# The first mLSTM head's q, k and v projections moved in front of the convolution tiles of a hybrid decoder step

## The chip, the cores and the metric

One core of a Trainium2 chip runs the whole step in one launch. The metric is the device time of a launch in microseconds (us), as the median of several runs; lower is better. The core has five engines that run at once, each with its own in-order instruction queue: TensorE (PE in the profile; PEld is its weight load), VectorE (DVE), ScalarE (ACT), GpSimd (POOL) and SyncE (SP, which here only issues DMAs).

## What is computed

One layer of a decoder for 512 prompt tokens and 8 x 8 sample tokens, so 576 columns of width 1024. Three groups of heads read the same normalised, modulated input; one output projection joins them, and an MLP follows. Cut to what matters:

```python
hn = (rmsnorm(x, norm1_w) * (1.0 + sc1) + sh1)           # sc, sh, g from adaLN of c
u = hn @ w_in
z, xbc, dt_raw, q, k, v, o, ig, fg, xr, gr = split(u)
xbc = silu(causal_conv(xbc, sconv0, w, b))               # 12 tiles of 128 channels
y_ssd = rmsnorm((ssd_chunked(xbc, softplus(dt_raw)) + xs * d) * silu(z))
hm = mlstm_chunked(q, k * 128 ** -0.5, v, ig, log_sigmoid(fg))   # 4 heads of 128
y_ml = rmsnorm(hm) * sigmoid(o)
y_lru = lru_scan(causal_conv(xr)) * gelu(gr)
x = x + g1 * (concat(y_ssd, y_ml, y_lru) @ w_out)
hn = rmsnorm(x, norm2_w) * (1.0 + sc2) + sh2
x = x + g2 * (square(relu(hn @ mlp_up)) @ mlp_down)
y = rmsnorm(x, final_norm_w)
```

All recurrent states are outputs too.

## The kernel before

Activations lie with channels on the 128 partitions and the 576 tokens along the free axis, in tiles from a pool of 54 places (`T`). A weight matrix is cut into 124 blocks of 1024 x 128; the host packs them in the order in which the kernel uses them, which it reads from the constant `ORDER`. For precision each block is split into two parts, `wh` (a copy on ScalarE, L150) and `wl` (the rest, L152, on POOL for blocks 7 to 32 and on VectorE for the others); each product is three matmuls (`mm_k`, L164), for two halves of 288 columns: 48 matmuls for a block of 8 k-steps. Raw blocks come by DMA on SP's queue (`w_load`, L128) into three buffers.

`unit` does one block: it loads and splits ahead, issues the matmuls into a pair of PSUM banks (`PG`, two pairs), calls `slot` after four k-steps, then the block's evacuation `evac`, then `slot` again. `slot` takes one step of each generator in `self.active`; the generators hold the work beside the projections: `gate_rows` (the gates' cumulative sums and maxima over tokens, mostly VectorE, up to a set of transposes at L596), `ssd(g)` (eight heads of the state space part, a chunk of 128 tokens in two steps), `mlstm(h, q, k, v)` (one mLSTM head), `ada_gen` (the later adaLN products) and others.

Evacuations differ. `ev_conv` (tiles of x, B and C, called "c") copies PSUM with three ScalarE operations (L611, L613, L614) into one of four row buffers `r`, scales on ScalarE into a second one (L620), adds three shifted products on VectorE (L626), a tanh on ScalarE (L649), and two VectorE operations give the result (L651, L653). `ev_copy` (q, k, v) is one ScalarE copy into a tile (L902). `ev_gates` starts `gate_rows` before the first of these blocks.

`start` does blocks 1 to 3 (tiles c8, c10, c0). `run` then does c1, c2, c3 (blocks 4 to 6), starts `ssd(0)`, and goes through `ORDER`: there "c" is a convolution tile, "m" the three blocks of an mLSTM head, "z", "x", "g" and "o" gate and recurrent-unit blocks. The first entries are c9 c11 c4 c5 c6 m0 c7 m1. An "m" appends the head's generator when its three blocks are done; when the last convolution is done `ssd(1)` is appended; `ada_gen` is appended at entry number `ADA_AT`. `ssd(0)` begins its chunks when `gate_rows` and its six convolution tiles are done. The head's first work is a broadcast load of `scr_nm` (L909, on SP's queue), then products of q and k.

The code only gives the order in which instructions are emitted. The final order in each engine's queue is drawn at build time by a scheduler that keeps dependences and buffers and models the instructions' times.

Of the kernel before, what the change touches and what calls it, by code (L numbers as in the profile page):

```python
# [67 lines left out]
class Kernel:  # L68
# [1200 lines left out]
    def run(self):  # L1269
# [11 lines left out]
        def inp(evac):  # L1281
            nonlocal blk
            self.unit([(blk, k, self.hn[k]) for k in range(KT)], evac)
            blk += 1
# [5 lines left out]
        convs = {9, 11, 4, 5, 6, 7}  # L1290
        for n, (kind, i) in enumerate(ORDER):
            if n == ADA_AT:
                self.active.append(self.ada_gen())
            if kind == "c":
                inp(lambda pg: self.ev_conv(pg, i))
                convs.remove(i)
                if not convs:
                    self.active.append(self.ssd(1))
            elif kind == "m":
                t = {}  # L1300
                inp(lambda pg: t.__setitem__("q", self.ev_copy(pg, "q")))
                inp(lambda pg: t.__setitem__("k", self.ev_copy(pg, "k", sc)))
                inp(lambda pg: t.__setitem__("v", self.ev_copy(pg, "v")))
                self.active.append(self.mlstm(i, t["q"], t["k"], t["v"]))
            elif kind == "x":
                if i == 0:
                    self.active.append(self.lru_setup())
                inp(lambda pg: self.ev_xr(pg, i))
                if i == 3:
                    self.active.append(self.lru())  # L1310
            elif kind == "g":
                inp(lambda pg: self.ev_gr(pg, i))
            elif kind == "z":
                if i == 0:
                    self.active.append(self.ssd_norm())
                inp(lambda pg: self.ev_z(pg, i))
            else:
                inp(lambda pg: self.ev_o(pg, i))
# [154 lines left out]
TODO = {0: [(0, 0)], 1: [(0, 1), (1, 0), (1, 1)], 2: [(0, 2), (1, 2)], 3: [(0, 3), (1, 3)], 4: [(0, 4), (1, 4), (2, 0), (2, 1)], 5: [(0, 5), (1, 5), (2, 2), (2, 3)], 6: [(0, 6), (1, 6), (2, 4), (2, 5)], 7: [(0, 7), (1, 7), (2, 6), (2, 7)]}  # L1473
GATES_FIRST = False
LOOKAHEAD = 4
ORDER = [(t[0], int(t[1:])) for t in "c9 c11 c4 c5 c6 m0 c7 m1 m2 z0 z1 x0 x1 x2 z3 z2 x3 g0 g1 z6 g2 g3 m3 z7 z5 z4 o0 o1 o2 o3".split()]
ADA_AT = 1
ON_ACT = ('mc_s', 'ssm_p', 'ssm_s')
PREP = 2
W_BUFS = 3  # L1480
# [23 lines left out]
def _layout(a):  # L1504
# [21 lines left out]
    blocks = [xt[8], xt[10], xt[0], xt[1], xt[2], xt[3]]  # L1526
    for kind, i in ORDER:
        blocks += [qt[i], kt[i], vt[i]] if kind == "m" else [{"c": xt, "x": rt, "g": gt, "z": zt, "o": ot}[kind][i]]
# [110 lines left out]
```

## Time and profile before

| | |
|---|---|
| three runs | 993.74, 996.15, 996.48 us (median 996.15) |
| the profiled execution | 995.4 us, of which its span, first to last instruction, 993.6 |
| granted TensorE clock, mean over the span | 0.987 |
| matmuls of line L164 in the chain that ended last | 66% of the span |
| HBM traffic | 119 GB/s over the span |

The profile is of one execution. "Busy" is the time in which an engine had an instruction in work; matmuls are pipelined, so a busy TensorE is not one at its peak. An idle time is put down to what ended it. A row of a timeline has the start, the length, the engine, the line, the operation, output and inputs and a count; in brackets, the idle time before it and what it waited for. In the page's rows of digits each digit is the busy share, in tenths, of one of 40 equal slices of 24.8 us.

### The profile page before, as it was taken

How to read it: one execution, taken by the hardware profiler on the slowest of the kernel's cores; microseconds unless marked ns; L12 is line 12 of the kernel's file. 1: busy time of each engine (PE TensorE's matmuls, PEld its weight loads, DVE VectorE, ACT ScalarE, POOL GpSimd, SP SyncE). 2: the span in 40 equal slices, each digit the busy share in tenths (PEclk: the TensorE clock that was granted, in tenths of full speed). 3: DMA queues.
4: the chain of work that ended last, by engine and by line, in shares of the span. 5: the costliest groups of instructions: out<-in, count | busy, mean ns of one | idle time of the engine just before them, and what ended most of it. 6: DMA issues, size and time to landing. Idle time of an engine off the chain costs nothing.

```text
span 993.6 us, 18146 instructions
## 1 busy us (share of the span) xinstructions
PE 959.5 (97%) x7369; PEld 904.1 (91%) x7370; DVE 590.2 (59%) x1180; ACT 399.8 (40%) x741; POOL 203.8 (21%) x220
## 2 busy tenths in 40 slices
PE   8999789889999999999999999999999999999996
PEld 5889778777788899999999999999999999999996
DVE  4669897887788377468444455533553355335544
ACT  3454744453646674345222234312441144114320
POOL 2836454532355532020000000000000000000032
PEclk8999999998999999999999999999999999999998
DMA  9721254654464333444222322222222222222202
GB/s 343 294 86 64 81 186 133 246 173 137 131 223 153 105 137 129 140 131 162 91 98 105 110 86 84 74 79 84 85 86 85 86 85 76 76 83 85 85 23 96
DMA packets 51220, 119.62 MB, mean 120 GB/s; under 512 B 6956, under 2 KB 17468, under 8 KB 51136
## 3 DMA queue, kind: packets, MB, share of 16 engines
q1 hardware_dynamic: 47024, 111.06, 32.7%
q10 hardware_dynamic: 3744, 6.85, 1.8%
q8 instruction: 58, 0.95, 0.4%
q0 software_dynamic: 368, 0.55, 0.2%
q14 instruction: 26, 0.21, 0.1%
HBM read 108.68 MB, written 9.76 MB: 119 GB/s over the span
## 4 chain that ended last, share of the span: by engine, by line
PE 76%; DVE 10%; ACT 4%; issue 3%; DMA 1%; POOL 0%; POOLq 0%; DVEq 0%; ACTq 0%
PE g L164 66%; DVE r L626 3%; PE adap L218 1%; PE g L1363 1%; DMA nmb<-scr_nm 1%; PE py L729 1%; PE lg L1129 1%; DVE att L707 1%; PE ps L734 1%; PE py L732 1%; DVE nmb L924 1%; DVE xbc L651 0%; DVE sp_e L494 0%; PE adas L228 0%; ACT r L620 0%
## 5 line engine op out<-in xcount | busy, mean ns | idle before, releaser
L150 ACT ACTIVATE wh<-raw 128x1024 fp32r<-128x1024 f32 x123 | 130.1, 1058 | 333.9 <-PE g L164 309.4
L164 PE MATMUL g<-hnh,wh 128*128 128x288 f32 x688 | 153.1, 302 | 10.1 <-ACT r L614 8.0
L164 PE MATMUL g<-hnh,wl 128*128 128x288 f32 x688 | 152.1, 299 | 0.6 <-DVE wl L152 0.6
L164 PE MATMUL g<-hnl,wh 128*128 128x288 f32 x688 | 151.8, 299 | 0.0
L152 DVE TENSOR_TENSOR wl<-raw,wh 128x1024 fp32r<-128x1024 f32 x97 | 118.7, 1225 | 29.5 <-ACT wh L150 29.4
L164 PEld LDWEIGHTS g<-hnh,wh 128*128 128x128 f32 x688 | 110.4, 189 | 19.3 <-ACT r L614 9.2
L164 PEld LDWEIGHTS g<-hnh,wl 128*128 128x128 f32 x688 | 111.6, 189 | 2.7 <-issue 1.2
L164 PEld LDWEIGHTS g<-hnl,wh 128*128 128x128 f32 x688 | 111.7, 189 | 0.8 <-issue 0.4
L164 PE MATMUL g<-h2h,wh 128*128 128x288 f32 (+1 forms) x512 | 110.9, 297 | 0.0
L164 PE MATMUL g<-h2l,wh 128*128 128x288 f32 (+1 forms) x512 | 110.9, 298 | 0.0
L164 PE MATMUL g<-h2h,wl 128*128 128x288 f32 (+1 forms) x512 | 110.0, 296 | 0.0
L307 DVE SCALAR_TENSOR_TENSOR xr<-g,modt,xr 128x288 f32<-128x288 f32 x38 | 19.7, 518 | 141.2 <-PE g L164 141.2
L164 PE MATMUL g<-hh,wl 128*128 128x288 f32 x480 | 102.9, 295 | 0.0
L164 PE MATMUL g<-hh,wh 128*128 128x288 f32 x480 | 102.5, 295 | 0.0
L164 PE MATMUL g<-hl,wh 128*128 128x288 f32 x480 | 102.4, 295 | 0.0
L1405 POOL TENSOR_SCALAR xr<-xr,vec 128x576 f32<-128x576 f32 (+2 forms) x8 | 15.2, 1900 | 383.8 <-ACT sqa L1237 363.4
L152 POOL TENSOR_TENSOR wl<-raw,wh 128x1024 fp32r<-128x1024 f32 x26 | 69.0, 2653 | 80.3 <-ACT wh L150 61.4
L164 PEld LDWEIGHTS g<-h2h,wl 128*128 128x128 f32 x512 | 83.4, 188 | 0.0
L164 PEld LDWEIGHTS g<-h2h,wh 128*128 128x128 f32 x512 | 83.1, 189 | 0.1
L164 PEld LDWEIGHTS g<-h2l,wh 128*128 128x128 f32 x512 | 83.0, 188 | 0.0
L164 PEld LDWEIGHTS g<-hh,wh 128*128 128x128 f32 x480 | 77.0, 188 | 0.0
L164 PEld LDWEIGHTS g<-hh,wl 128*128 128x128 f32 x480 | 77.0, 188 | 0.0
(399 smaller groups left out, 1652.7 us busy)
## 6 DMA issues: line engine op xcount, KB each, us to landing
raw<-w SPq DMA_DIRECT2D x124, 512.0 KB, 3.5
ada<-ada SPq DMA_DIRECT2D x32, 512.0 KB, 5.6
ada<-ada SPq DMA_DIRECT2D x32, 256.0 KB, 5.9
cumb<-scr_cum SPq DMA_DIRECT2D x16, 256.0 KB, 5.6
s<-s SPq DMA_DIRECT2D x16, 256.0 KB, 4.7
ssm_s<-s ACTq DMA_DIRECT2D x16, 256.0 KB, 2.9
x<-x SPq DMA_DIRECT2D x8, 288.0 KB, 4.7
xr<-x SPq DMA_DIRECT2D x8, 288.0 KB, 3.9
```

Of the source, the lines that this page charges most:

```text
L150: nc.scalar.activation(hi, raw, AF.Copy)
L152: eng.tensor_tensor(lo, raw, hi.bitcast(FT), op=OP.subtract)
L164: self.nc.tensor.matmul(pg.h[h][:m, :e], w(k), xx[:, h * HALF:h * HALF + e], start=start and n == 0, stop=stop and n == 2)
L218: nc.tensor.matmul(ps[32 * j:32 * j + 32, :256], self.cs[:, k, :], ks(k), start=k < 4, stop=k >= 4)
L307: self.nc.vector.scalar_tensor_tensor(dst[:, :HALF], pg.h[0][:, :HALF], gate[:, 0:1], x[:, :HALF], op0=OP.mult, op1=OP.add)
L626: nc.vector.scalar_tensor_tensor(a[:, :n], r[:, j:j + n], wcols[:, j:j + 1], a[:, :n], op0=OP.mult, op1=OP.add)
L707: self.eng("att").tensor_scalar(E[:, h * 128:(h + 1) * 128], cums[h2][:, h * 128:(h + 1) * 128], self.col1[:, c, hd:hd + 1], 0.0, op0=OP.a ...
L729: nc.tensor.matmul(o, xdt[:, h * 64:(h + 1) * 64], att[h // 4][:, hs], start=True, stop=not c)
L732: nc.tensor.matmul(o, S[:, h * 64:(h + 1) * 64], ce[h // 4][:, hs], start=False, stop=True)
L734: nc.tensor.matmul(pst, cb[:, 128:256], xend[:, :512], start=True, stop=True)
L924: self.eng("nmb").tensor_scalar(E[:, tk(c)], nmb[:, tk(c)], ecol(c), 0.0, op0=OP.add, op1=OP.min)
L1405: self.eng("fin").tensor_scalar(x, x, self.v("fnw")[:, o:o + 1], None, op0=OP.mult)
```

## The change

The head's three blocks become the first entry of `ORDER`, the head's generator is not started when they are done but after c6 (the entry after which it started before), and `ada_gen` is appended before the first entry, not before the second.

```diff
             if kind == "c":
                 inp(lambda pg: self.ev_conv(pg, i))
                 convs.remove(i)
+                if i == M0_AFTER:
+                    self.active.append(self.mlstm(*first))
                 if not convs:
                     self.active.append(self.ssd(1))
             elif kind == "m":
...
                 inp(lambda pg: t.__setitem__("v", self.ev_copy(pg, "v")))
-                self.active.append(self.mlstm(i, t["q"], t["k"], t["v"]))
+                if i:
+                    self.active.append(self.mlstm(i, t["q"], t["k"], t["v"]))
+                else:
+                    first = i, t["q"], t["k"], t["v"]
...
-ORDER = [(t[0], int(t[1:])) for t in "c9 c11 c4 c5 c6 m0 c7 m1 m2 z0 z1 x0 x1 x2 z3 z2 x3 g0 g1 z6 g2 g3 m3 z7 z5 z4 o0 o1 o2 o3".split()]
-ADA_AT = 1
+ORDER = [(t[0], int(t[1:])) for t in "m0 c9 c11 c4 c5 c6 c7 m1 m2 z0 z1 x0 x1 x2 z3 z2 x3 g0 g1 z6 g2 g3 m3 z7 z5 z4 o0 o1 o2 o3".split()]
+ADA_AT = 0
+
+M0_AFTER = 6
```

Five convolution tiles (c9, c11, c4, c5, c6) now stand between v0 and the head's start; the sixth, c7, followed the head before and still does. The block count at which the head's generator is appended, eleven blocks after the start, is the same.

## The prediction

> **What bounds the kernel now.** I read the page first: the engines' busy shares, the 40 slices and the chain that ended last.
>
> ```profile
> span 993.6 us, 18146 instructions
> PE 959.5 (97%) x7369; PEld 904.1 (91%) x7370; DVE 590.2 (59%) x1180; ACT 399.8 (40%) x741; POOL 203.8 (21%) x220
> PE   8999789889999999999999999999999999999996
> DVE  4669897887788377468444455533553355335544
> PE 76%; DVE 10%; ACT 4%; issue 3%; DMA 1%; POOL 0%; POOLq 0%; DVEq 0%; ACTq 0%
> ```
>
> TensorE is the bound: 993.6 - 959.5 = 34 us of idle time in the whole span, nearly all of it in the first 15 slices, where the DVE row is also at its highest. An average over the span says nothing of a change that reorders work near slice 4, so I cut the span at the places where the work changes character: the table by stretches, whose columns are the stretch, its length, then busy time of PE, PEld, DVE, ACT and POOL with their counts, the granted clock, the DMA share and GB/s.
>
> ```profile
> 60.00:99.00 39.00, 38.20 (x287) 37.98 (x288) 35.49 (x43) 21.10 (x42) 21.23 (x29) 1.00 0.15 55
> 99.00:114.00 15.00, 9.36 (x58) 8.84 (x58) 14.68 (x30) 9.39 (x23) 5.62 (x10) 0.89 0.23 74
> 114.00:168.00 54.00, 50.93 (x434) 44.26 (x434) 45.15 (x104) 27.59 (x54) 26.05 (x18) 1.00 0.52 156
> 168.00:245.00 77.00, 68.92 (x556) 57.67 (x555) 61.90 (x148) 36.99 (x89) 33.64 (x29) 0.96 0.52 173
> 245.00:400.00 155.00, 151.83 (x1181) 136.62 (x1180) 110.11 (x241) 93.71 (x212) 62.34 (x56) 1.00 0.43 147
> 400.00:582.00 182.00, 182.00 (x1421) 176.47 (x1420) 92.52 (x182) 63.95 (x111) 10.17 (x20) 1.00 0.35 118
> ```
>
> After 400 us TensorE never idles: whatever is won or lost before is carried to the end. From 60 to 99 it idles 0.80 us. From 99 to 114 it idles 5.64 of 15 us while VectorE works 14.68 of 15: this is the one place where VectorE is the bound. From 114 to 168 TensorE idles 3.07 us and VectorE 8.85. The timeline of TensorE and the waits in that window show what the 5.64 us are.
>
> ```profile
> PE g L164 <- ACT r L614: 5.6, 2, 4.3
> 98.69 0.43 PE L164 MATMUL g<-hnl,wh 128*128 128x288 f32 x2
> 98.95 0.42 PE L164 MATMUL g<-hnh,wl 128*128 128x288 f32 x2
> 103.65 0.70 PE L164 MATMUL g<-hnh,wh 128*128 128x288 f32 x2 [4.28 <-ACT r L614]
> 104.14 0.68 PE L164 MATMUL g<-hnl,wh 128*128 128x288 f32 x2
> 106.30 1.05 PE L596 MATMUL ca<-vec,cs 128*128 128x128 f32 x4
> 113.74 0.53 PE L164 MATMUL g<-hnh,wh 128*128 128x288 f32 x2 [1.36 <-ACT r L614]
> 118.91 0.66 PE L596 MATMUL ca<-vec,cs 128*128 128x128 f32 x4 [0.27 <-ACT cs L587]
> 132.82 1.26 PE L729 MATMUL py<-att,xdt 128*64 128x128 f32 x16 [1.53 <-DVE att L711]
> ```
>
> Two waits of `g`, 4.28 and 1.36 us, both on L614, the last of the three copies with which `conv` takes a projection out of its PSUM pair. There are two pairs, so block n+2 waits for the copies of block n. Why the copies were late stands in the timelines of VectorE (first four rows) and ScalarE (last three).
>
> ```profile
> 101.92 0.66 DVE L651 SCALAR_TENSOR_TENSOR xbc<-r,r 128x512 f32<-128x512 f32 x1
> 102.51 0.21 DVE L653 SCALAR_TENSOR_TENSOR xbc<-r,r 128x64 f32<-128x64 f32 x1
> 107.55 2.81 DVE L626 SCALAR_TENSOR_TENSOR r<-r,cwh,r 128x600 f32<-128x600 f32 x1
> 111.17 0.69 DVE L651 SCALAR_TENSOR_TENSOR xbc<-r,r 128x512 f32<-128x512 f32 x1
> 98.78 0.68 ACT L531 ACTIVATE cs<-sp 16x576 f32<-16x576 f32 x1 [4.91 <-DVE sp L499]
> 102.83 0.40 ACT L611 ACTIVATE r<-g 128x288 f32<-128x288 f32 x1
> 112.93 0.40 ACT L611 ACTIVATE r<-g 128x288 f32<-128x288 f32 x1
> ```
>
> The copies write a row buffer `r`, of which there are four, two to a convolution. The copy of c11 starts at 102.83, right after VectorE finished an older convolution (L653 at 102.51); the copy of c4 starts at 112.93, after the next one (L651 at 111.17 and its L653). Those last steps sat behind the gate rows' operations in VectorE's in-order queue. So the chain is: gate rows and convolutions on one engine, row buffers, PSUM pair, TensorE.
>
> **The change part by part.** Count projections ("blocks") from the first after the start: c1 c2 c3 are 4 to 6. Before, 7 to 14 are c9 c11 c4 c5 c6 q0 k0 v0; after, q0 k0 v0 c9 c11 c4 c5 c6. c7 is block 15 in both, and the head's own generator starts at the same count, so its loads and arithmetic keep their place. No operation is added or removed: 18146 instructions stay, only their order differs.
>
> *The two stalls.* Blocks 7, 8 and 9 now leave PSUM by one copy each into an ordinary tile, not into `r`:
>
> ```profile
> L902 ACT ACTIVATE q<-g x4: 632/645/646, 145.2 to 392.6; 128x576 f32<-128x576 f32 x4
> L626 DVE SCALAR_TENSOR_TENSOR r<-r,cwh,r 128x600 f32<-128x600 f32 x33 | 34.5, 1057 | 3.5 <-ACT r L620 3.2
> L651 DVE SCALAR_TENSOR_TENSOR xbc<-r,r 128x512 f32<-128x512 f32 x11 | 9.2, 840 | 3.6 <-ACT r L649 3.5
> L653 DVE SCALAR_TENSOR_TENSOR xbc<-r,r 128x64 f32<-128x64 f32 x11 | 2.4, 219 | 0.0
> ```
>
> 0.65 us of ScalarE, nothing of VectorE, against 3 x 1.06 + 0.84 + 0.22 = 4.2 us of VectorE for a convolution (the last three rows are groups from 60 to 168 us). The stall of 4.28 us, where block 10 waited for block 8, goes: block 8 is now k0. So does the 1.36 us before block 11. With the first goes the slow start behind it: pairs of matmuls start 0.26 us apart at 98.69 and 0.49 at 103.65, about 11 matmuls until 106.1, at 0.11 us extra 1.2 us; the four transposes at 106.30 took 1.05 us, their twins at 118.91 0.66, 0.4 more. Together 4.28 + 1.36 + 1.6 = 7.2 us by which TensorE could stand ahead.
>
> [...]
>
> *What is late next.* VectorE's work does not go away. Of the convolutions that move back, c9 and the first two steps of c11 were done before 114: five L626, one L651, one L653, 5 x 1.06 + 0.84 + 0.22 = 6.3 us. In the new order TensorE would reach the same block boundary at 114 - 7.2 = 106.8; until then VectorE has 35.49 + 14.68 - 6.3 = 43.9 us to do in 46.8, which fits. From there to the end of block 14 and the fourth chunk of `ssd(0)` (168 before) it has 45.15 + 6.3 = 51.5 us, where TensorE has 54. So the stretch ends at 168 - 7.2 = 160.8 if TensorE sets it, and at 106.8 + 51.5 + 8.85 = 167.1 if VectorE keeps every gap that it had. Some of these gaps go, since they wait for TensorE, which is now ahead; others go with ScalarE's answers and stay. I take the middle, 164.0: **a gain of 4.0 us** between the ends 0.9 and 7.2.
>
> The row at 107.55 shows an L626 of 2.81 us, against a median of 0.84, while POOL's split at 107.14 ran:
>
> ```profile
> 107.14 2.58 POOL L152 TENSOR_TENSOR wl<-raw,wh 128x1024 fp32r<-128x1024 f32 x1 [3.27 <-ACT wh L150]
> L626 DVE SCALAR_TENSOR_TENSOR r<-r,cwh,r x33: 739/842/2987, 61.5 to 134.2; 128x600 f32<-128x600 f32 x33
> ```
>
> I let the lengthened steps move with their mean. [...]
>
> *Queues.* The weight loads keep their number, size and place; only which block lies in them differs. ScalarE: the three copies now stand among the gate rows' activations. If k0's copy were queued behind L531 (98.78, above) it would end at 98.78 + 0.68 + 0.65 = 100.1, and block 10, ready at 99.2, would start 0.9 us late; I cost this at nothing, between 0 and 0.9, since k0 is ready at about 92.7, in the 4.91 us in which ScalarE did nothing. SP: the head's loads and raw loads keep their order. `ada_gen` starts one block earlier, so its first pair of loads comes ahead of the `decb` load, behind which SP stood in before:
>
> ```profile
> 109.74 0.33 SPq L128 DMA_DIRECT2D raw<-w  x1
> 117.86 0.33 SPq L590 DMA_DIRECT2D decb<-scr_ends  x1
> 118.31 0.93 SPq L667 DMA_DIRECT2D cumb<-scr_cum  x2
> 120.31 1.11 SPq L238 DMA_DIRECT2D ada<-ada  x2
> 174.09 0.37 SPq L909 DMA_DIRECT2D nmb<-scr_nm  x1
> ```
>
> That is 1.1 us of issuing moved from behind `cumb` to ahead of `decb`, in time where the queue was waiting for `scr_ends` anyway (109.74 to 117.86): nothing, or at worst 1.1 us on `cumb`. Each adaLN product is the same work one block sooner. POOL's queue: the conv's small copies move with their convolution, behind the same splits; nothing. Tiles: q, k and v take three of 54 places where three of the later convolutions' outputs lay before; nothing.
>
> *The head.* q, k and v are ready some 60 us before it (block 9 ends near 99, the head's first load is issued at 174). It still waits for its `nmb` load (issued at 174.09), which SP issues after weight loads that wait for splits, which wait for TensorE's blocks; that load comes earlier by as much as block 14 does. So I carry the 4.0 us whole. What is not shown is how the rest of the order is redrawn: TensorE idles 8.1 us from 168 to 245 and 3.2 from 245 to 400, and a new order can move some of this either way. I take nothing, with 3 us either way for the range, a quarter of it.
>
> **Sum.** The profiled execution took 995.4 us (span 993.6 and 1.8 around it): 995.4 - 4.0 = 991.4. The median of the runs shown, 996.15, lies 0.75 above it and would give 992.1; I say 991.8.
>
> **The rivals.**
>
> *VectorE takes it back.* The stretch from 114 keeps all its gaps and ends at 167.1, or c6's leftovers push the `ssd` sample part: a gain of 0.9 or nothing, 994.5 to 996. For it: 51.5 us in 54 is 95% busy, and VectorE's work depends on ScalarE's answers. Against it: 45.15 us in 54 ran with only 3.07 us of TensorE idle.
>
> *The whole gain and more.* No new stall, 7.2 us, and one or two of the 3.07 us of idle time from 114 to 168 filled by work that is ready: 986 to 988. Against it: that stretch gets 6.3 us more VectorE work.
>
> *Stalls come back larger (slower).* c4, c5 and c6 now leave PSUM while `ssd(0)` runs its chunks on VectorE. A chunk holds the queue for a run of operations:
>
> ```profile
> 137.94 0.28 DVE L693 TENSOR_TENSOR cbm<-cb,vec 128x128 f32<-128x128 f32 x1
> 144.07 0.69 DVE L743 TENSOR_TENSOR S<-S,ps 128x512 f32<-128x512 f32 x1
> ```
>
> From 137.94 to 144.76 that is one chunk, 6.8 us with one convolution's last two steps in it (0.84 + 0.22 by the means above), about as long as a block's 48 matmuls at 0.13 us (6.4). If last steps L651 land behind a chunk as they landed behind the gate rows, the next copy waits for `r`, and TensorE stalls as at 99: 4.28 + 1.6 = 5.9 us each. One such stall leaves 1.3 of the 7.2; from two on it is slower: 11.8 - 7.2 = 4.6, 1000; with three, 1006.
>
> *The order written is not the order issued.* Instructions are ordered by a scheduler that also models their times: the transposes of the gate rows and the copies do not stand where the code emits them. If it draws the copies of q0, k0, v0 late, block 9 or 10 stalls as before and the time is 995 to 996. This counts with "takes it back".
>
> **How the numbers follow.** Forecast (989 to 994): 0.45. Taken back (994 to 998): 0.28. More (below 989): 0.12. Slower (above 998): 0.15. The range 986 to 1000 takes in all but the far ends of the last two. A measurement of this kernel can tell about 0.3%, 3 us, from no change, so faster is below 993.2 and slower above 999.1. The forecast puts 0.40 of its 0.45 below 993.2 and the third case its 0.12: faster 0.52. Slower than 999.1: 0.14. The rest, 0.34, is the same.
>
> **What would show it.** Right: between 92 and 112 us no wait of `g` L164 for L614 above 1 us and a granted clock of 1.00 from 99 to 114; the L902 copies of q0, k0, v0 between 86 and 101; VectorE at 9 tenths from 107 to 160; the head's `nmb` load issued near 170. Wrong: a wait for L614 of 3 us or more between 115 and 165, or waits of `py` for `att` (1.53 us at 132.82 now) that grow; or a head that starts no earlier although the first stall is gone.

## The result and the profile after

| | before | after |
|---|---|---|
| median | 995.1 us (993.74 to 996.48, 4 runs) | 1014.2 us (1013.46 to 1017.08, 4 runs) |
| ratio | | 1.016, 95% interval 1.0121 to 1.0199 |
| profiled execution, its span | 995.4, 993.6 us | 1013.46, 1011.7 us |
| mean granted clock | 0.987 | 0.976 |

The changed kernel is slower by 19 us by the medians (1014.2 / 995.1 = 1.019; the recorded ratio, whose estimate is not the quotient of the medians, is 1.016), outside the range. All ratios and differences in per cent below are recorded ratios. The page of after says in its first part what kind of time it is.

```profile
span 1011.7 us, 18141 instructions
PE 967.9 (96%) x7370; PEld 909.6 (90%) x7370; DVE 595.8 (59%) x1180; ACT 401.8 (40%) x741; POOL 200.8 (20%) x220
```

TensorE idles 1011.7 - 967.9 = 43.8 us, 9.7 more than before, and is busy 8.4 us longer with the same matmuls, which goes with the lower granted clock (0.976, not 0.987). The table by stretches of after, with the cuts of the prediction (length, busy PE, PEld, DVE, ACT, POOL, then clock, DMA share, GB/s), says where.

```profile
60.00:99.00 39.00, 32.26 (x240) 31.81 (x240) 35.05 (x46) 20.00 (x40) 18.72 (x28) 0.97 0.16 55
99.00:114.00 15.00, 10.42 (x74) 8.80 (x75) 8.37 (x22) 10.64 (x22) 4.52 (x5) 0.73 0.33 109
114.00:168.00 54.00, 53.96 (x440) 47.16 (x440) 47.65 (x97) 26.77 (x55) 23.38 (x21) 1.00 0.46 137
168.00:245.00 77.00, 65.01 (x505) 53.65 (x501) 60.60 (x134) 33.45 (x83) 33.38 (x30) 0.93 0.52 163
245.00:400.00 155.00, 147.86 (x1151) 132.22 (x1151) 112.22 (x256) 92.46 (x211) 63.41 (x56) 0.98 0.44 148
```

From 60 to 99 TensorE now idles 6.74 us (0.80 before), and from 99 to 114 the clock is 0.73 (0.89). From 114 to 168 it idles 0.04 us (3.07 before): there the change did what it was to do. Then it loses 3.9 us against before from 168 to 245, and 4.0 from 245 to 400. So there are three places. The next tables count the projection matmuls (L164) issued by 103, 170 and 290 us; first before, then after.

```profile
0.00:103.00 103.00, 60.13 (x432) 57.73 (x432) 0.95 0.54 195
0.00:170.00 170.00, 103.17 (x729) 98.57 (x730) 0.96 0.50 173
0.00:290.00 290.00, 161.78 (x1124) 152.50 (x1124) 0.96 0.52 176
```

```profile
0.00:103.00 103.00, 54.10 (x384) 51.69 (x384) 0.92 0.52 190
0.00:170.00 170.00, 98.93 (x706) 94.87 (x706) 0.94 0.49 168
0.00:290.00 290.00, 155.44 (x1075) 147.59 (x1076) 0.94 0.50 166
```

After is a whole block (48) behind at 103 us, 23 at 170 and 49 at 290. Before issues 297 of them in the 67 us between 103 and 170, one in 0.226 us, so the gap is 10.8 us, then 5.2: a new loss ahead of 103 us, half of it won back by 170, and lost once more by 290.

**The first loss.** The waits of TensorE (total, times, longest) and its timeline in after:

```profile
PE ca L596 <- DVE cs L541: 10.2, 1, 10.2
PE g L164 <- ACT r L614: 2.4, 2, 2.1
```

```profile
92.91 0.42 PE L164 MATMUL g<-hnh,wl 128*128 128x288 f32 x2
103.58 1.08 PE L596 MATMUL ca<-vec,cs 128*128 128x128 f32 x4 [10.25 <-DVE cs L541]
104.81 1.94 PE L218 MATMUL adap<-ada,cs 128*32 128x256 f32 x16
...
204.10 1.07 PE L218 MATMUL adap<-ada,cs 128*32 128x256 f32 x16
```

The waits of `g` for L614 have gone but for the start's 2.4 us. In their place the transposes of the gate rows, which in before ran at 106.30 without a wait, stand in TensorE's queue at the end of block 8 and wait 10.25 us for VectorE. The 16 small products behind them take 1.94 us at a granted clock of 0.50 (104.80 to 106.75), and 1.07 us a hundred microseconds later at 1.00 (204.10 to 205.20). Why a queue holds the transposes there, ahead of block 9, shows ScalarE's timeline.

```profile
100.66 0.68 ACT L553 ACTIVATE d<-cs 4x576 f32<-4x576 f32 x1
104.70 0.60 ACT L598 ACTIVATE col<-ca 128x512 f32<-128x512 f32 x1 [3.36 <-PE ca L596]
105.19 0.64 ACT L902 ACTIVATE q<-g 128x576 f32<-128x576 f32 x1
```

q0 is block 7 (7 x 48 = 336 matmuls, done by 87 us in after), but its one copy runs at 105.19, behind the transposes' own copy (L598). Until then its PSUM pair is taken, block 8 holds the other, and block 9 can't start. It looks as if the build, modelling TensorE as free after block 8, put the transposes there. In the code q0's tile is asked for after some of the gate rows' tiles (d, mx, mt), out of the same pool of 54 places; read from the built queues, its copy got no place ahead of theirs.

**The second and third loss** begin at 170 us. SyncE's queue before and after, at the second `ssd`'s sample part (start, length):

```profile
241.83 0.33 SPq L128 DMA_DIRECT2D raw<-w  x1
243.80 0.80 SPq L238 DMA_DIRECT2D ada<-ada  x2
248.19 0.59 SPq L760 DMA_DIRECT2D cumf<-scr_cum  x1
```

```profile
252.98 15.03 SPq L128 DMA_DIRECT2D raw<-w  x2
268.10 0.59 SPq L760 DMA_DIRECT2D cumf<-scr_cum  x1
268.79 1.24 SPq L763 DMA_DIRECT2D cump<-scr_cum  x2
```

In before one weight load stands ahead of the `cumf` load; in after two in a row, the second of which waits 14.3 us for a split on GpSimd (L152) that frees its buffer, and `cumf` starts 20 us later.

### The profile page after: what moved, and what is told of

Its sections match the earlier page's. It is cut to its first block, busy times and chain, and to the rows that moved or that the text cites. A ratio compares the mean times of both kernels' runs of the same rounds, so it can differ in the third digit from the quotient of the medians.

```text
span 1011.7 us, 18141 instructions
## 1 busy us (share of the span) xinstructions
PE 967.9 (96%) x7370; PEld 909.6 (90%) x7370; DVE 595.8 (59%) x1180; ACT 401.8 (40%) x741; POOL 200.8 (20%) x220
## 4 chain that ended last, share of the span: by engine, by line
PE 72%; DVE 13%; ACT 3%; issue 3%; DMA 1%; POOL 1%; SPq 0%; POOLq 0%; ACTq 0%; DVEq 0%
PE g L164 63%; DVE r L626 3%; PE adap L218 1%; PE g L1368 1%; DVE att L707 1%; DVE xbc L651 1%; DVE att L711 1%; PE lg L1129 1%; DMA nmb<-scr_nm 1%; DVE num L1059 1%; DVE y L736 1%; DVE bst L804 1%; DMA cump<-scr_cum 0%; DVE sp_e L494 0%; PE pn L971 0%
## 5 line engine op out<-in xcount | busy, mean ns | idle before, releaser
L164 PE MATMUL g<-hnh,wh 128*128 128x288 f32 x688 | 155.5, 306 | 5.5 <-ACT r L614 2.4
L164 PE MATMUL g<-hnh,wl 128*128 128x288 f32 x688 | 152.7, 301 | 0.6 <-DVE wl L152 0.6
L164 PE MATMUL g<-hnl,wh 128*128 128x288 f32 x688 | 150.7, 299 | 0.0
L152 DVE TENSOR_TENSOR wl<-raw,wh 128x1024 fp32r<-128x1024 f32 x97 | 118.8, 1225 | 39.1 <-ACT wh L150 39.0
L164 PEld LDWEIGHTS g<-hnh,wh 128*128 128x128 f32 x688 | 112.5, 192 | 14.8 <-issue 6.0
L164 PEld LDWEIGHTS g<-hnh,wl 128*128 128x128 f32 x688 | 112.7, 191 | 2.5 <-issue 1.0
L164 PEld LDWEIGHTS g<-hnl,wh 128*128 128x128 f32 x688 | 112.6, 191 | 1.2 <-issue 0.8
L164 PE MATMUL g<-h2l,wh 128*128 128x288 f32 (+1 forms) x512 | 111.2, 298 | 0.0
L164 PE MATMUL g<-h2h,wh 128*128 128x288 f32 (+1 forms) x512 | 111.0, 298 | 0.0
L164 PE MATMUL g<-h2h,wl 128*128 128x288 f32 (+1 forms) x512 | 110.7, 298 | 0.0
L164 PE MATMUL g<-hh,wl 128*128 128x288 f32 x480 | 102.7, 295 | 0.0
L164 PE MATMUL g<-hl,wh 128*128 128x288 f32 x480 | 102.5, 295 | 0.0
L164 PE MATMUL g<-hh,wh 128*128 128x288 f32 x480 | 102.5, 295 | 0.0
L152 POOL TENSOR_TENSOR wl<-raw,wh 128x1024 fp32r<-128x1024 f32 x26 | 67.6, 2599 | 98.6 <-ACT wh L150 89.5
L164 PEld LDWEIGHTS g<-h2l,wh 128*128 128x128 f32 x512 | 83.8, 189 | 0.0
L164 PEld LDWEIGHTS g<-h2h,wl 128*128 128x128 f32 x512 | 83.6, 189 | 0.0
L164 PEld LDWEIGHTS g<-h2h,wh 128*128 128x128 f32 x512 | 83.3, 188 | 0.1
L164 PEld LDWEIGHTS g<-hl,wh 128*128 128x128 f32 x480 | 76.9, 188 | 0.0
L164 PEld LDWEIGHTS g<-hh,wh 128*128 128x128 f32 x480 | 76.9, 188 | 0.0
```

The lines of the kernel that those rows point to most:

```text
L152: eng.tensor_tensor(lo, raw, hi.bitcast(FT), op=OP.subtract)
L164: self.nc.tensor.matmul(pg.h[h][:m, :e], w(k), xx[:, h * HALF:h * HALF + e], start=start and n == 0, stop=stop and n == 2)
```

## The experiments

Ratios are against the kernel before on the same chip, with the 95% interval; 0.1% is 1 us.

| run | what it is | median, us | ratio | interval |
|---|---|---|---|---|
| e1_own_tiles | after, own tiles | 1008.46 | 1.0092 | 1.0052 to 1.0132 |
| e2_ada_as_before | after, generator later | 1007.98 | 1.0094 | 1.0058 to 1.0130 |
| f1_own_and_ada | after, both | 999.17 | 1.0015 | 0.9987 to 1.0042 |
| e3_before_own_tiles | before, own tiles | 993.63 | 0.9953 | 0.9926 to 0.9979 |
| g4_before_ada0 | before, generator earlier | 1001.19 | 1.0043 | 1.0009 to 1.0077 |
| e4_before_xbc_own | before, other own tiles | 998.31 | 1.0010 | 0.9987 to 1.0032 |
| f4_between | blocks half way | 1001.80 | 1.0023 | 0.9995 to 1.0052 |
| f2_before_short | before, ten products out | 998.34 | 1.0000 | 0.9971 to 1.0030 |
| f3_both_short | f1, ten products out | 994.51 | 0.9961 | 0.9935 to 0.9987 |
| g1_own_short | e3, ten products out | 1001.46 | 1.0039 | 1.0013 to 1.0065 |
| g2_both_onact | f1, five products off VectorE | 997.73 | 0.9998 | 0.9972 to 1.0024 |
| g3_own_onact | e3, five products off VectorE | 1000.08 | 1.0027 | 1.0006 to 1.0049 |
| h1_own_pool | e1, loads on GpSimd's queue | 1013.96 | 1.0117 | 1.0076 to 1.0158 |
| h2_own_ada_pool | f1, loads on GpSimd's queue | 1016.84 | 1.0159 | 1.0119 to 1.0198 |
| h3_before_own_53 | e3, 53 places | 996.36 | 0.9959 | 0.9928 to 0.9990 |
| h4_both_53 | f1, 53 places | 996.27 | 0.9977 | 0.9952 to 1.0003 |

### Two parts undone: the copies' tiles and the generator

Own tiles: the first three results of `ev_copy` (q0, k0, v0) get three places of a tag of their own.

```diff
-        t = self.T(name)
+        if self.qkv0 < 3:
+            t = self.tpool.tile([128, TW], FT, name=self.name(name), tag="qkv0", bufs=3)[:, :NT]
+            self.qkv0 += 1
+        else:
+            t = self.T(name)
```

The generator later: it is appended after q0's block, so behind as many blocks as before the change.

```diff
                 inp(lambda pg: t.__setitem__("q", self.ev_copy(pg, "q")))
+                if not i:
+                    self.active.append(self.ada_gen())
...
-ADA_AT = 0
+ADA_AT = -1
```

e1 has the first, e2 the second, f1 both; e3 is the kernel before with the first, g4 the kernel before with `ADA_AT = 0` alone.

> The changed order, with q0, k0 and v0 in three tiles of their own and no longer in the shared pool of 54. Theory (a copy into the shared pool is ordered behind the gate rows' tiles, which were asked for earlier, so q0 stays in PSUM until the gate rows are far on): q0's copy starts near 87 us, not 105; TensorE's wait of 10.25 us before the gate rows' transposes is below 3 us; block 9 ends near 100 and the time is 1000 to 1003 us if what was lost after 170 us stays lost, 988 to 992 if that came from the same cause. Rival (the transposes themselves were placed too early, whatever q0 does): the wait of 8 to 10 us stays and the time is 1010 to 1015. Rival (VectorE's backlog of convolutions costs the time, not this wait): the early wait goes but TensorE is stalled again by 160 us, time 1008 to 1014.

> The changed order with the adaLN generator started after the same number of blocks as before (after q0, not ahead of it). Theory: it has no part in the early wait, which stays at about 10 us; time 1011 to 1016. Rival (the earlier adaLN products and loads cost the time, in the early wait or after 170 us): 995 to 1006.

> The kernel after with both single edits of the first set: the three tiles of the first head in places of their own, and the adaptation generator begun after q0's block, behind as many blocks as before. Theory of two separate losses (the early wait, worth about 5.7 us of the time, and the earlier generator, worth about 6.2 us): the two add up, the time comes to 1014.2 - 5.7 - 6.2 = about 1002, still 5 to 8 us above the kernel before, and the lag behind before is near 0 or below at the 750th matmul of the g tiles and grows by 5 to 8 between there and the 900th. Rival (both edits cure the same loss, by another draw of the order): the time stays at about 1008. Second rival (nothing else is wrong): 990 to 996, level with before or better.

> The kernel before with q0, k0 and v0 in three tiles of their own: the control for the three extra places. Theory: these copies come long after the gate rows there, nothing waits for them, 992 to 997 us. Rival (three more places help by themselves): below 990.

> The kernel before with one edit of the change alone: the adaptation generator begun one block earlier (before c9, not after it). Theory that the generator's place moves SyncE's queue as in the kernel after, where two weight loads stand in a row ahead of the second chunk's cumf and cump loads: these loads start 10 us or more later than in before (248 and 254.6 us) and the time rises by about 6 us, to 999 to 1003. Rival (the generator's place costs only together with the moved blocks): 993 to 997, with cumf near 248.

With own tiles the copy runs 12 us earlier, and the wait shrinks; e1's timeline of ScalarE and its waits of TensorE:

```profile
92.87 0.63 ACT L907 ACTIVATE q<-g 128x576 f32<-128x576 f32 x1
```

```profile
PE ca L597 <- DVE cs L542: 2.5, 1, 2.5
```

Its count of projections at 103 us is 3 behind before, not 48:

```profile
0.00:103.00 103.00, 60.64 (x429) 58.45 (x430) 0.92 0.53 190
```

Nothing but the place of three results was edited, so the late copy was the cause of the 10.25 us wait. The edit is worth 0.68% without and 0.79% with the later generator (after to e1, e2 to f1), some 7 us; but also 0.47% in the old order, where no such wait stood and the same copy moves from 145.2 to 131.8 us. How much of the 7 us is the wait's own is therefore not shown; in the two profiled executions e1 has lost its lead over after again by 290 us (1076 and 1075 projections). e3 is the one kernel of these that is shown to beat the kernel before. Its table by stretches beside that of before, 140 to 160 us (first e3):

```profile
140.00:160.00 20.00, 20.00 (x182) 16.74 (x181) 13.05 (x37) 8.18 (x14) 7.07 (x4) 1.00 0.49 138
```

```profile
140.00:160.00 20.00, 18.73 (x173) 15.69 (x172) 17.48 (x49) 8.96 (x17) 5.58 (x4) 1.00 0.64 189
```

The generator is worth 0.66% and 0.77% in the new order (after to e2, e1 to f1) and 0.43% in the old one (before to g4): 4 to 8 us for an entry moved by one block. The place can be read from the counts: g4 is level with before at 245 us (960 projections each), 20 behind at 290 and 45 at 400; e1 is level with f1 at 170 (753 and 748) and 29 behind at 290. SyncE's queue in g4 and in f1 around `cumf`:

```profile
239.65 17.40 SPq L128 DMA_DIRECT2D raw<-w  x2
257.15 0.58 SPq L760 DMA_DIRECT2D cumf<-scr_cum  x1
```

```profile
245.34 0.33 SPq L129 DMA_DIRECT2D raw<-w  x1
247.30 0.84 SPq L239 DMA_DIRECT2D ada<-ada  x2
251.70 0.59 SPq L761 DMA_DIRECT2D cumf<-scr_cum  x1
```

After, e1 and g4, the three with the earlier generator that are compared here, have the two weight loads in a row; before, e2 and f1 don't. Both parts together are 1.45% of the 1.6% (after to f1); f1's interval includes no change.

### Own places for the results of the other late copies (e4)

```diff
-        t = self.T("xbc")
+        if i in (3, 9, 11):
+            t = self.tpool.tile([128, TW], FT, name=self.name("xbc"), tag="xbc0", bufs=3)[:, :NT]
+        else:
+            t = self.T("xbc")
```

> The kernel before with the results of c3, c9 and c11 in three tiles of their own. Theory (the same ordering by the shared pool put c3's last two VectorE steps behind the gate rows' scan): the stall of 4.28 us at 99 us is below 1.5 us, and the time 988 to 992. Rival (VectorE was simply full there): the stall stays at 3 to 5 us and the time at 993 to 997.

The kernel before with the results of c3, c9 and c11 in own places. The 4.28 us stall that the change was to remove is gone, by another way, and e4's waits of TensorE from 60 to 125 us show what came for it:

```profile
PE ca L596 <- DVE cs L541: 7.6, 1, 7.6
PE g L164 <- ACT r L614: 0.3, 1, 0.3
```

No gain (1.0010). The account that fits is that whoever reaches the gate rows first waits for them, the copies of a convolution or the transposes: the same exchange as in after, without the change.

### Is it VectorE's load? (f2, f3, g1, g2, g3, f4)

f2, f3 and g1 leave out two of three shifted products (L626) in c9, c11, c4, c5 and c6, so that these convolutions have two taps in place of four: 10.6 us of VectorE by the mean of 1.06 us, though its busy time over the launch fell by only 6.5 (before to f2), 9.8 (f1 to f3) and 5.1 us (e3 to g1); g2 and g3 keep the result and move the last of them to ScalarE and GpSimd. In g2 and g3 the second added line is `rest = "dda"`. f4 has the order "c9 c11 m0 c4 c5 c6 c7" with own tiles.

```diff
         first, *rest = CONV
+        if self.short:
+            rest = rest[:1]
...
+        self.short = i in (9, 11, 4, 5, 6)
         a, th = self.conv(pg, None, self.cwh[:, 4 * i:4 * i + 4], self.cwh[:, 48 + i:49 + i],
```

> The kernel before, with two of the three shifted products of the convolutions c9, c11, c4, c5 and c6 left out, 10 instructions of about 1.06 us on VectorE; those convolutions then have two taps in place of four, and the output is not the reference's. It is the partner of the next run. VectorE has gaps before and after the moved stretch: 992 to 997, a change of 0 to -3 us, if VectorE's queue bounds little of before; 985 to 990 if it bounds the whole stretch.

> The first kernel of this set with the same ten instructions left out. Theory that the moved convolution work piles up on VectorE at 160 to 190 us and is what the changed order loses there: 10.6 us less of it takes the pile away, and this kernel comes out 0 to 5 us below the previous one (the kernel before with the same left out). Rival (the loss is not VectorE's amount of work but which work stands first in the queues and where tiles come free): it stays 5 to 8 us above the previous one.

> The kernel before with the three tiles in places of their own and the same ten convolution products left out as in f2 and f3 (two taps in place of four in c9, c11, c4, c5 and c6; the output is not the reference's). It differs from f3 by the place of the three blocks and of nothing else, as the kernel before with own tiles (0.9953) differs from f1 (1.0015). Theory that the amount of VectorE work at 160 to 240 us is what the moved order loses: the difference of 0.6% shrinks or turns, so this kernel lies at 992 to 996, not below f3 by more than 0.2%. Rival (the ten products cost the same in either order): it lies about 0.6% below f3, near 988 to 990.

> The moved order with own tiles and the later generator (f1), and in c9, c11, c4, c5 and c6 the last shifted product made by ScalarE and added by GpSimd in place of VectorE: five instructions of about 1.06 us off VectorE, the output that of the reference. Theory (VectorE's pile): about half of what f3 gained over f1, 996 to 998, ratio 0.997 to 1.000. Rival (GpSimd's wide additions hold VectorE up, and ScalarE's queue delays the copies): 1000 to 1006.

> The kernel before with own tiles and the same five products moved from VectorE to ScalarE and GpSimd: the partner of the run above. In this order VectorE has gaps at 140 to 200 us, so little is to be won: 992 to 996, level with the kernel before with own tiles (0.9953). Rival (GpSimd and ScalarE become the bound): 998 to 1004.

> The kernel before with the three tiles in places of their own and the first head's blocks after c9 and c11, ahead of c4, c5, c6 and c7; the head begins where it did, the adaptation generator too. Blocks 7 and 8 are convolutions again, so the gate rows keep two blocks with little else on VectorE, while four convolutions in place of six come late. Theory (VectorE's pile in proportion to the convolutions that come late): between the kernel before with own tiles (ratio 0.9953) and the first kernel of this set, 992 to 999. Rival (the early wait comes back, since the copies of blocks 9 to 11 are again cheap on VectorE but the gate rows are late): 1000 to 1008.

In the moved order less VectorE work helps: f1 to f3 is -0.54%, f1 to g2 -0.17% (the latter inside the intervals). In the old order the same edits cost time: e3 to g1 +0.86%, e3 to g3 +0.74%, although ten or five operations are gone from the engine. An amount of work can't explain both signs. f2, without own tiles, changes nothing. f4 is no middle: its q copy is at 107.6 us, and the wait of `g` for the conv copies is back at 4.3 us. The theory of VectorE's load alone falls; each of these edits also draws the later order anew, and g2 and g3 add work to ScalarE and GpSimd.

### Is it SyncE's queue? (h1, h2)

```diff
-        nc.sync.dma_start(cumf[:64, :512].rearrange("p (h t) -> p h t", h=8),
+        nc.gpsimd.dma_start(cumf[:64, :512].rearrange("p (h t) -> p h t", h=8),
```

The same for `cump` and the `ssd` states (L757), in e1 (h1) and f1 (h2).

> The kernel after with own tiles (e1), and the loads of cumf, cump and the ssd states (L761, L764, L757) issued from GpSimd's queue in place of SyncE's. Theory that the earlier generator costs its 6 to 7 us because two weight loads stand in a row ahead of these loads on SyncE (in e1 cumf starts at 266.5 us, behind a weight load that waits 16.8 us): with another queue the wait is gone, cumf starts by 250 to 255 and the time falls from about 1008 to 1000 to 1003. Rival (the generator's place costs through the order on TensorE and VectorE, and the late load is only its trace): the time stays at 1006 to 1010. Second rival (GpSimd's queue delays the loads as much): cumf no earlier than 262 and the time unchanged; then nothing is told apart.

> The same edit on the kernel with own tiles and the later generator (f1), where only one weight load stands ahead of cumf: by the theory of SyncE's queue little is to be won, 996 to 1001. Rival (the loads are better off on GpSimd's queue whatever the generator does): 992 to 995, as large a gain as in the run above.

h1's timeline of GpSimd:

```profile
259.26 2.36 POOL L153 TENSOR_TENSOR wl<-raw,wh 128x1024 fp32r<-128x1024 f32 x1 [10.24 <-ACT wh L151]
261.56 0.78 POOL L761 DMA_DIRECT2D cumf<-scr_cum  x1
```

On GpSimd the load queues behind the split of a weight block, which waited 10.24 us, and gets only 4.9 us earlier (266.48 in e1); the control h2 becomes 1.4% slower than f1 by the edit alone. This tells nothing of SyncE's part. That the generator's place costs 4 to 8 us is shown; that it does so through the two weight loads goes with the traces compared above, and isn't shown.

### How much is a redrawn order worth? (h3, h4)

```diff
-N_TILES = 54
+N_TILES = 53
```

> The kernel before with own tiles (e3, ratio 0.9953) and 53 places in the shared pool in place of 54: a control, since one place less means nothing to the early stretch but draws the later order anew. If the ratios of e3 and f1 differ because of the moved blocks, this one stays within 0.3% of 0.9953; if a redrawn order alone is worth some 5 us, it lies anywhere between 0.993 and 1.004.

> f1 (moved blocks, own tiles, later generator; ratio 1.0015) with 53 places: the partner of the control. By a loss of the moved blocks themselves it lies 0.6% above the control; by a redrawn order alone the difference can have either sign.

h3 stays where e3 was. h4 comes down to 0.9977, 0.18% above h3, with overlapping intervals. Four pairs now differ, in the code, in the place of the blocks and in nothing else: f1 to e3 +0.62%, h4 to h3 +0.18%, g2 to g3 -0.29%, f3 to g1 -0.78%. The moved blocks themselves, once copies and generator are put right, have no sign that these runs could settle.

### What the traces have in common

The prediction's gain was there in h4 and f1 and was then lost. The counts of projection matmuls in f1, as above:

```profile
0.00:170.00 170.00, 108.30 (x748) 104.06 (x748) 0.95 0.50 171
0.00:290.00 290.00, 160.81 (x1105) 152.75 (x1105) 0.95 0.52 172
```

At 170 us f1 is 19 matmuls ahead of before (4.3 us at 0.226), at 290 us 19 behind. Part of that lead comes from the own tiles; e3, its partner in the old order, at 170 us:

```profile
0.00:170.00 170.00, 104.96 (x736) 100.13 (x736) 0.95 0.51 171
```

Against the partner f1 is 12 ahead, 2.7 us. The other pairs are 37 (h4 to h3), 20 (g2 to g3) and 3 (f3 to g1) ahead, so the moved blocks lead in all four at 170 us, by 0.7 to 8.4 us, in one profiled execution each. TensorE's timeline of h4, which is 44 ahead at 170 us, shows where such a lead goes.

```profile
182.57 0.38 PE L165 MATMUL g<-hnh,wl 128*128 128x288 f32 x1
186.64 0.50 PE L830 MATMUL pu<-xst,bst 96*128 96x512 f32 x1 [3.69 <-DVE modt L230]
...
196.91 0.69 PE L976 MATMUL pn<-v,nmb 128*128 128x130 f32 x4
...
200.28 0.51 PE L165 MATMUL g<-hnh,wh 128*128 128x288 f32 x2
```

At 182.57 the 17th block ends, and no projection is issued until 200.28, when the first head's products (`pn`) are through. In all 18 kernels exactly 816 = 17 x 48 projection matmuls stand ahead of the first `pn`. Projections are the work that fills TensorE; when the 17th block is done early, as here, nothing is left to fill with until the head's chain through VectorE, ScalarE and DMA has come through. So the start of the first `pn` may tell more than an earlier lead; before and after:

```profile
195.75 0.69 PE L971 MATMUL pn<-v,nmb 128*128 128x130 f32 x4
```

```profile
205.10 0.71 PE L971 MATMUL pn<-v,nmb 128*128 128x130 f32 x4
```

and in the pair g2 and g1, moved and old order with less on VectorE:

```profile
192.78 0.69 PE L979 MATMUL pn<-v,nmb 128*128 128x130 f32 x4
```

```profile
200.36 1.21 PE L979 MATMUL pn<-v,nmb 128*128 128x130 f32 x4
```

The head's first load comes no earlier either. In f1, which leads at 170 us, it is issued 8 us later than in before (174.09):

```profile
182.00 0.37 SPq L914 DMA_DIRECT2D nmb<-scr_nm  x1
```

Over sixteen kernels (all but h1 and h2) the start of `pn` and the ratio go together with a correlation of 0.86; the count of projections at 170 us gives -0.42. Over all eighteen it is 0.68, and h2 is the exception to keep in mind: its `pn` starts at 195.99 us, as early as in before, but it is the slowest but one; it is level with before at 245 us (960 projections) and 116 behind at 400. Without the three slow ones of the sixteen (after, e1, e2) it is 0.66. That was read afterwards, and no edit moved the chain alone: a likely account of where the lead goes, not a shown one.

## Why the prediction was wrong

- **The two stalls: right.** The waits for L614 at 99 and 113.7 us are gone, and from 114 to 168 TensorE idles 0.04 us, not 3.07.
- **The queues, "I cost this at nothing, between 0 and 0.9": the step that failed.** It asked when k0's data would be ready and which activations stood in the queue before. It didn't ask for q0's copy, of the block before k0's, nor where the new order would put it. The copy came 18 us after its block and held a PSUM pair, and what came of it was 10.25 us of idle time and a clock of 0.73 from 99 to 114. The own tiles that removed this wait won some 7 us (e1, f1); the control e3, without such a wait, won 4.7 by the same edit, so the wait's own share of the time stays open. The rival "The order written is not the order issued" named it, and priced it at a stall "as before"; it was larger, since VectorE's gate rows were still not done.
- **`ada_gen` one block earlier, "nothing, or at worst 1.1 us": mis-sized.** 6.6 and 7.7 us in the new order, 4.3 in the old. I looked at the loads beside it, at 100 us; the cost began between 170 and 290 us, in g4 behind 245. By which path is open.
- **VectorE's debt, a gain of 4.0 between 0.9 and 7.2: the sign was right for the place where it was worked out, the size is not settled.** With the two other parts put right, f1 is 4.3 us ahead of before at 170 us, but that this is so near 4.0 is luck: against their partners the four kernels with moved blocks lead by 0.7 to 8.4 us. What failed is that I took it for a gain of the time, because "whatever is won or lost before is carried to the end": that holds from 400 us on, while a lead at 170 us first meets the first head's chain, which doesn't start earlier by itself (`nmb` is loaded at 178.48 in after, at 174.09 in before, and in f1, which leads at 170, only at 182.00). I had set the `nmb` load near 170 as a sign, and "a head that starts no earlier" as what would make me wrong; it was so.
- **The rest of the order redrawn, 3 us either way: too small.** Five edits of before that were to win time or do nothing (e3, e4, f2, g1, g3) lie between 0.9953 and 1.0039, 8.6 us from end to end.
- **The slower rival** had the right sign and the wrong place: no wait behind `ssd` chunks grew to 5.9 us between 115 and 165; the loss was ahead of 107 us and behind 170.
- **Slips that change little.** TensorE fell idle at 103.65 - 4.28 = 99.37 us, not at 99.2, so the bound on the queues was 0.7, not 0.9; the VectorE work that moves is 6.36 us, so 6.4. And "never idles" after 400 us holds up to the launch's end: from 960 us to the end before idles 8.0 us, after 8.1 in its last 36.7.

## What to carry to other kernels

A copy that frees a scarce buffer is as late as the place that it writes to: before counting on "one copy in place of three", look which pool the result comes from, what was asked of that pool before it, and what the queue will put in the gap. When a block of filler work is moved forward, find the next point where the filler ends and something else must come through (here the first head's `pn` behind block 17): a lead that reaches that point early can be lost there. And where a scheduler draws the order, do a few edits that should do nothing, to learn how much the drawing alone is worth, before reading a cause into half a per cent.

## What was not expected of the hardware

The operation for which the transposes waited was itself long: 2.18 us in after, 0.752 for the same one in before, beside which no GpSimd split ran. VectorE's timeline in before, then the timelines of VectorE and GpSimd in after:

```profile
105.11 0.75 DVE L541 TENSOR_TENSOR cs<-de,sp 16x576 f32<-16x576 f32 x1
```

```profile
101.25 2.18 DVE L541 TENSOR_TENSOR cs<-de,sp 16x576 f32<-16x576 f32 x1
```

```profile
100.16 2.66 POOL L152 TENSOR_TENSOR wl<-raw,wh 128x1024 fp32r<-128x1024 f32 x1 [0.91 <-ACT wh L150]
```

GpSimd's split ran from 100.16 to 102.82, beside the first 1.57 us of L541, which ended 0.61 us after it, at 103.43. Both lengths of L541 were measured; why it was longer here, no run shows. The difference of the two lengths is 1.4 us of the 10.25.
